# One decoder step on one core: the page stream pinned to its program order, and the second output projection moved in between FFN slices

## The chip, the core and the metric

The kernel runs on one core of one Trainium2 chip. The metric is the device time of one launch in microseconds (us). TensorE (PE in the profile, PEld for its weight loads), VectorE (DVE), ScalarE (ACT), GpSimd (POOL) and the DMA queue of SyncE (SP) each work through their own instruction stream in order and wait for each other by semaphores.

## The reference

One layer of a hybrid decoder, for a prompt of 1024 tokens and for 8 sequences of 8 new tokens each, which also attend to 8192 cached tokens. In short (widths: model 1024, FFN 2816):

```python
def layer_forward(h, p, pos, gla_s0, conv_prev, attend, lw):
    u = rmsnorm(h, lw['g_mix']) @ lw['w_in']
    gq, gk, gv, gg, ga, mq, mkv, mkr = split(u)
    ...                                        # o_gla: gated linear attention, 4 heads
    ckv = rmsnorm(mkv, lw['mla_g_kva']); krope = rope(rmsnorm(mkr, lw['mla_g_kr']), pos)
    k_m, v_m = latent_to_kv(ckv, krope, ...)   # 8 heads, per-head norm of the keys
    o_mla = attend(q_m, k_m, v_m)              # prompt: causal; sample: 64 cached pages of 128 per sequence
    h = h + concat([o_gla, o_mla]) @ lw['w_o']
    y, conv_new = conv_ffn(rmsnorm(h, lw['g_ffn']), conv_prev, lw)   # (silu(conv3(n @ gate)) * (n @ up)) @ down
    h = h + y
    return h + (p @ lw['ple_w_proj']) * sigmoid(rmsnorm(h, lw['g_ple']) @ lw['ple_w_gate']), ...
```

All data are float32. A product is made as three products of rounded halves (high x high, high x low, low x high; helper `mm3`), so that float32 precision is kept at the faster rate of the rounded type.

## The kernel before

The work has two strands. The **page stream** (`cache_stream`) is the sample sequences' attention over the cache: 64 blocks of 1024 cached tokens, eight for each sequence, called pages here. A page is gathered by indirect DMA (`stage_load`, two pages ahead, three buffers), transposed (`pre`, tile `ctp`, L518) and split into `cTh` and `cTl`; `main` multiplies it with the key weights and the queries (tile `ks`), ScalarE squares and copies the result out of PSUM (`csq`, `sn`); `stage_b` makes the key norm and the scores, `stage_c1` the softmax (`mt`, Exp, `phl`), `stage_pv` the product with the latents (`cpv`). The generator yields twice for each page, with half a page of `main` in each step, and `stage_b` of a page runs one page later, `stage_pv` two.

The **dense strand** (`dense`) is all else: input projections and latents in two halves of 512 prompt tokens (`prompt_half`), linear attention (`gla_sample`, `gla_prompt`), causal prompt attention (`prompt_attention`, tiles `S`, `t`, `o`), then for the first half of the prompt the output projection (`wo_half(0)`, sums in `ps_dn`) and the FFN (`ffn_half(0)`): 22 slices of 128 hidden columns, each with gate and up products (`ff_chunk`, tile `ps_gu`, 48 matmuls of 512 columns) and, for every two slices, the product with the down weights (`down`, 48 matmuls). Before the FFN the rows are normalised, transposed and split again (`renormer`: `row_scale`, `xnorm`, `turned`, tile `pt`).

A loop at the end of the program interleaves the strands in program order. The dense generator yields how many microseconds of TensorE it has just emitted; a step of the stream is emitted whenever the sum of these passes a due time, which each step moves on by 4.4 x `PACE[part]`. The parts are the projections (0 to 3), linear attention (4, 5), prompt attention (6), `wo_half(0)` (7) and the first FFN half (8). In the kernel before, the last step falls among the 22nd slice.

Program order is not the order that runs. At build time a scheduler places the instructions on the engines, by a simulated timeline: of what is ready, that which stands first in program order goes first, and later work may be pulled forward where an engine would otherwise be idle. `tc.keep_in_program_order(ins)` adds one constraint: `ins` is not placed ahead of the instruction that was traced before it on its engine.

After both strands have ended, the stream's memory is released and used for the second half's tiles (pools `psT` and `xr`: the rows `h1` and `hs`, the operand `X1`). Then come `wo_half(1)` (second half of the prompt and the sample rows; `down_sample`, tile `ps_ds`), its renormalisation, `ffn_half(1)` and the last gate (`ple_unit`). TensorE's sums take PSUM tiles in turn from `pd` (three banks) in the first half, and from `both` (`pd`, `pm`, `p2`, six banks) in the second.

Of the kernel before, what the change touches and what calls it, by code (L numbers as in the profile page):

```python
# [8 lines left out]
F32 = mybir.dt.float32  # L9
F32R = mybir.dt.float32r  # L10
# [5 lines left out]
PSUM = bass.MemoryType.PSUM  # L16
DRAM = bass.MemoryType.DRAM

P = 128
D = 1024  # L20
# [4 lines left out]
R = NB * TS  # L25
H = 8
DFF = 2816
PACE = [2.0, 1.5, 2.2, 1.65, 1.6, 1.0, 1.45, 1.37, 1.34]
SP = 50
PLAN = ([0], [], [1, 2, 3])  # L30
VIAP = 20
# [1 line left out]
VIAQ = 40  # L33
LOP = 1
NF = DFF // P
EPS = 1e-6
NEG = -1e30
SCALE = 96.0 ** -0.5
# [7 lines left out]
def step_kernel(ctx: ExitStack, tc: tile.TileContext, A):  # L46
    nc = tc.nc
    pe, act, dve, pool, sp = nc.tensor, nc.scalar, nc.vector, nc.gpsimd, nc.sync
# [9 lines left out]
    ident = ctile([P, P], F32, "ident")  # L58
# [119 lines left out]
    ph1 = ctx.enter_context(ExitStack())  # L178
# [18 lines left out]
    z = {}  # L197
# [310 lines left out]
    def pre(o, g0):  # L508
        buf = o.b % 2
        if g0 == 0:  # L510
            if o.bi == 0:
                seq_setup(o.b)
            o.sr = cp.tile([P, 9, 64], F32, tag="sr", name="sr", bufs=2)
        gn = min(4, o.nt - g0)
        craw = newc if g0 == 8 else o.craw[:, g0:g0 + 4]
        tp = pm([P, 4, P], "ctp")
        for i in range(gn):
            pe.transpose(tp[:, i, :], craw[:, i, :], ident)  # L518
        cTh = cp.tile([P, 4, P], F32R, tag="cTh", name="cTh", bufs=2)
# [792 lines left out]
    cs = cache_stream()  # L1312
    done = object()

    def dense():
        for hf in range(2):
            z["part"] = 2 * hf
            if hf:
                z["gla"] = gla_weights()
            yield from prompt_half(hf)  # L1320
        den.close()
        wa2 = const.tile([17, 256], F32, tag="gtile", name="wa2")
        sp.dma_start(wa2[0:1], A["gla_b_a"])
        sp.dma_start(wa2[1:17], A["gla_w_a2"][0])
        with ExitStack() as s2:
            g, g2 = (s2.enter_context(tc.tile_pool(name=nm, bufs=2, reuse_waits="tile")) for nm in ("g", "g2"))
            z["part"] = 4
            sample = gla_sample(g, wa2, *z["gla"])
            for n, w in enumerate(gla_prompt(g2, wa2, *z["gla"])):
                yield w  # L1330
                if n > GS0:
                    z["part"] = 5
                    w2 = next(sample, None)
                    if w2 is not None:
                        yield w2
            for w in sample:
                yield w
        gsx.close()
        with ExitStack() as s2:
            ap = s2.enter_context(tc.tile_pool(name="ap", bufs=2, reuse_waits="tile"))  # L1340
            z["part"] = 6
            yield from prompt_attention(ap)
        z["part"] = 7
        open_dense()
        yield from wo_half(0)
        z["part"] = 8
        yield from ffn_half(0)


    chunks, wgu = {}, {}  # L1350
# [3 lines left out]
    def open_dense():  # L1354
# [29 lines left out]
    def hrows(t):  # L1384
        return z["h"][t // 4][:, t % 4] if t < NT else z["hs"]
# [9 lines left out]
    def down(grp, bank, hf, after=None):  # L1395

        for t in range(4):
            tt = slice(t * P, (t + 1) * P)
            for f in range(2):
                cs = slice(f * 512, (f + 1) * 512)  # L1400
                ps = bank([P, 512], "ps_dn")
                for i, c in enumerate(grp):
                    sh, sl, _, wdh, wd = chunks[c]
                    mm3(ps, sh[:, tt], sl[:, tt], wdh[:, cs], wd[:, cs], i == 0, i == len(grp) - 1)
                h = hrows(4 * hf + t)[:, cs]
                dve.tensor_tensor(h, h, ps, ALU.add)  # L1406
            if after is not None:
                after(4 * hf + t)
            yield 2.7
# [15 lines left out]
    def row_scale(t):  # L1425
# [4 lines left out]
        for f, s_ in enumerate((s0, s1)):  # L1430
# [3 lines left out]
        pool.tensor_tensor(z["rs"][:rows, t:t + 1], s0, mhalf[:rows, 0:1], ALU.pow)  # L1434

    XN = {(False, 0): "sca", (False, 1): "cca", (False, 2): "guh", (False, 3): "gul",
          (False, 4): "cca", (False, 5): "sca", (False, 6): "guh", (False, 7): "gul", (False, 8): "pth",
          (True, 0): "pth", (True, 1): "ptl", (True, 2): "pth", (True, 3): "ptl",
          (True, 4): "cca", (True, 5): "guh", (True, 6): "cca", (True, 7): "gul", (True, 8): "cca"}

# [40 lines left out]
    def renormer(again, bank, lag=2):  # L1481

        last = []

        def step(t):
            if len(last) == lag or (t is None and last):
                turned(*last.pop(0), bank, again)
            if t is None:
                return
            row_scale(t)  # L1490
            xn = xn_halves(t, again)
            xnorm(t, xn, pool if (VIAQ if again else VIAP) >> t & 1 else dve)
            last.append((t, xn))
        return step
# [21 lines left out]
    def wo_half(hf):  # L1516

        bank = z["both"] if hf else pd
        if hf:
            sp.dma_start(z["hs"], A["x_sample"].rearrange("b t d -> (b t) d"))  # L1520
        for t in range(4 * hf, 4 * hf + 4):
            sp.dma_start(hrows(t), A["x_prompt"][0, t * P:(t + 1) * P, :])
        for g in range(4):
            grp = (2 * g, 2 * g + 1)
            for c in grp:
                wo_chunk(c, hf)
            if g == 0 and not hf:
                conv_weights()
                sp.dma_start(z["gb"], A["g_ffn"][0].partition_broadcast(P))
            if g == 1 and hf:  # L1530
                conv_state()
            if hf:
                down_sample([chunks[c][2:] for c in grp], bank)
            step = renormer(False, p2t if hf else pd) if g == 3 else None
            if g == 3:
                ff_weights(0, hf)
                if hf:
                    step(NT)
            yield from down(grp, bank, hf, step)
        step(None)  # L1540
        step(None)


    def columns(src, kc, lo_eng=None):
# [2 lines left out]
    def ff_weights(f, hf):  # L1547
        fs = slice(f * P, (f + 1) * P)
        wgu[f] = tuple(columns(A[nm][0][:, fs], 8, pool if not hf and nm == "ffn_w_up" or f < LOP else dve)
                       for nm in ("ffn_w_gate", "ffn_w_up"))  # L1550
# [63 lines left out]
    def ffn_half(hf, hooks={}):  # L1614
        bank = z["both"] if hf else pd
        for g in range(0, NF, 2):
            for f in (g, g + 1):
                yield from ff_chunk(f, hf)
            after = hooks[g]() if g in hooks else None
            yield from down((g, g + 1), bank, hf, after)  # L1620
            if hf:
                down_sample([chunks[c][2:] for c in (g, g + 1)], bank)

    dn = dense()
# [12 lines left out]
    ph1.close()  # L1637


    psT = ctx.enter_context(tc.tile_pool(name="psT", bufs=2, space=PSUM, reuse_waits="tile"))  # L1640

    def p2t(shape, name):
        return psT.tile(shape, F32, tag="t", name=name)

    def p2(shape, name):
        return psT.tile(shape, F32, tag="b", name=name, bufs=1)

    turn = [0]

# [2 lines left out]
        return (pd, pm, pd, pm, pd, p2)[turn[0]](shape, name)  # L1652

    z["both"] = both
    xr = z["xr"] = ctx.enter_context(tc.tile_pool(name="xr", bufs=1, side="right", reuse_waits="tile"))
    wf, fb, fw = z["wf"], z["fb"], z["fw"]
    z["h"].append(xr.tile([P, 4, D], F32, name="h1"))
    z["X"].append(xr.tile([P, 8, 2, 512 + R], F32R, name="X1"))
    hs = z["hs"] = xr.tile([R, D], F32, name="hs")
    cout = z["cout"] = xr.tile([P, 18, NF], F32, name="cout")  # L1660

    def gain(nm):
        sp.dma_start(z["gb"], A[nm][0].partition_broadcast(P))
# [1 line left out]
    def run(it):  # L1665
        for _ in it:
            pass
# [41 lines left out]
    def ple_gate(c):  # L1709
# [28 lines left out]

    hooks = {8 + 2 * t: early(t) for t in range(4)}
    hooks[NF - 2] = last_hook  # L1740
    run(ffn_half(1, hooks))
    step = steps[1]
    step(NT)

# [109 lines left out]
```

## Time and profile before

| what | value |
|---|---|
| median of 3 runs | 2309.7 us (2306.23 to 2310.57) |
| profiled execution | 2310.78 us, span 2309.1 us |
| granted TensorE clock, mean | 0.985 |
| busy: TensorE, VectorE, ScalarE, GpSimd | 2205.9, 1567.9, 1403.6, 1023.9 us |
| DMA | 207.67 MB, mean 90 GB/s |

The profile shows one execution. A matmul's duration there is its time in the pipeline; consecutive ones overlap, so that their rate is read from counts in a stretch, not from the mean duration. The granted clock is the share of TensorE's full clock that the chip allowed in a stretch.

### The profile page before, as it was taken

To read this page: it belongs to the slowest core of one execution; us is meant where nothing else is said; L and a number is where in the kernel's file an instruction comes from. 1 tells how busy PE (TensorE), PEld (TensorE's weight loads), DVE (VectorE), ACT (ScalarE), POOL (GpSimd) and SP (SyncE) were. 2 spreads that over 40 slices of the span, in tenths; PEclk is the share of its full clock that TensorE was granted. 3 is DMA by queue.
4 is the path that set the end of the run, shared out by engine and by line. 5 is a ranking of instruction groups with operands and counts; after the bars stand their busy time and mean duration, and the time that the engine had idled before them with its cause. 6 is when DMAs were issued, how large, how long until landed. Compare 5 with 4: busy or idle time off the path is not lost.

```text
span 2309.1 us, 38976 instructions
## 1 busy us (share of the span) xinstructions
PE 2205.9 (96%) x13855; PEld 1952.7 (85%) x13855; DVE 1567.9 (68%) x2590; ACT 1403.6 (61%) x3758; POOL 1023.9 (44%) x1223
## 2 busy tenths in 40 slices
PE   7999999999999999999999999999798999999999
PEld 6889888788888888878788888878667999999999
DVE  5765684778878788878755666666677656666642
ACT  6666666768788888876655467767635323232431
POOL 6665675766867777664532234444313000000100
PEclk9999999999999999999999999999898999999999
DMA  5343343323322122143332232222142223232131
GB/s 185 110 133 112 102 152 124 100 69 96 95 75 64 58 58 60 40 143 110 90 93 85 85 100 79 78 78 67 39 138 74 85 81 91 75 92 74 52 116 39
DMA packets 228531, 207.67 MB, mean 90 GB/s; under 512 B 41326, under 2 KB 190291, under 8 KB 228339
## 3 DMA queue, kind: packets, MB, share of 16 engines
q1 hardware_dynamic: 216051, 163.23, 23.5%
q0 software_dynamic: 12288, 41.95, 5.8%
q8 instruction: 111, 1.82, 0.3%
q14 instruction: 81, 0.66, 0.1%
HBM read 178.56 MB, written 26.53 MB: 89 GB/s over the span
## 4 chain that ended last, share of the span: by engine, by line
PE 54%; ACT 5%; DVE 5%; DMA 4%; POOL 3%; issue 2%; POOLq 0%; SPq 0%; DVEq 0%; ACTq 0%
PE ps_gu L137 6%; PE ps_gu L138 6%; PE ps_gu L139 6%; PE ps_dn L137 4%; PE ps_dn L138 4%; PE ps_dn L139 4%; PE ks L137 3%; PE ks L139 2%; PE ks L138 2%; PE ps_pg L139 1%; PE ps_pg L137 1%; PE ps_pg L138 1%; PE cpv L605 1%; PE ctp L518 1%; DMA stg<-ffn_w_gate 1%
## 5 line engine op out<-in xcount | busy, mean ns | idle before, releaser
L542 ACT ACTIVATE csq<-ks 128x256 f32<-128x256 f32 x1040 | 389.2, 400 | 91.1 <-PE ks L139 85.1
L547 DVE TENSOR_REDUCE css<-csq 128x16 f32<-128x1024 f32 (+1 forms) x264 | 315.9, 1197 | 81.0 <-ACT csq L542 75.4
L138 PE MATMUL ps_gu<-X,guh 128*128 128x320 f32 (+2 forms) x1056 | 349.0, 331 | 0.0
L139 PE MATMUL ps_gu<-X,gul 128*128 128x320 f32 (+2 forms) x1056 | 348.4, 330 | 0.0
L137 PE MATMUL ps_gu<-X,guh 128*128 128x320 f32 (+2 forms) x1056 | 348.3, 331 | 0.1
L137 PE MATMUL ks<-mv0h,cTh 128*128 128x256 f32 (+1 forms) x780 | 249.2, 320 | 10.6 <-ACT sn L544 7.3
L138 PE MATMUL ks<-mv0l,cTh 128*128 128x256 f32 (+1 forms) x780 | 225.8, 291 | 0.0
L139 PE MATMUL ks<-mv0h,cTl 128*128 128x256 f32 (+1 forms) x780 | 222.4, 292 | 0.0
L139 PEld LDWEIGHTS ps_gu<-X,gul 128*128 128x128 f32 x1056 | 199.9, 189 | 14.4
L138 PEld LDWEIGHTS ps_gu<-X,guh 128*128 128x128 f32 x1056 | 199.7, 189 | 14.6
L137 PEld LDWEIGHTS ps_gu<-X,guh 128*128 128x128 f32 x1056 | 199.3, 189 | 15.0 <-ACT X L116 0.4
L116 ACT CAST guh<-stg 128x512 fp32r<-128x512 f32 x188 | 111.4, 620 | 149.2 <-PE ps_gu L138 70.4
L137 PE MATMUL ps_dn<-wdh,sh 128*128 128x512 f32 x480 | 188.4, 400 | 3.6 <-DVE h L1406 2.6
L138 PE MATMUL ps_dn<-wdl,sh 128*128 128x512 f32 x480 | 189.1, 394 | 0.0
L139 PE MATMUL ps_dn<-wdh,sl 128*128 128x512 f32 x480 | 179.7, 395 | 0.0
L1406 DVE TENSOR_TENSOR h<-h,ps_dn 128x512 f32<-128x512 f32 x240 | 154.4, 680 | 34.3 <-PE ps_dn L139 33.9
L137 PEld LDWEIGHTS ks<-mv0h,cTh 128*128 128x128 f32 x780 | 148.1, 190 | 33.2 <-ACT sn L544 16.6
L574 POOL TENSOR_TENSOR chl<-craw,chl 128x1024 fp32r<-128x1024 f32 x64 | 141.8, 2215 | 62.7 <-ACT chl L573 62.1
L117 DVE TENSOR_TENSOR gul<-stg,guh 128x512 fp32r<-128x512 f32 x138 | 94.5, 708 | 101.3 <-ACT guh L116 97.6
L138 PEld LDWEIGHTS ks<-mv0l,cTh 128*128 128x128 f32 x780 | 148.3, 190 | 7.8 <-issue 1.3
L593 POOL TENSOR_TENSOR phl<-sn,phl 128x512 fp32r<-128x512 f32 (+1 forms) x64 | 85.8, 1340 | 147.5 <-ACT phl L592 147.3
L139 PEld LDWEIGHTS ks<-mv0h,cTl 128*128 128x128 f32 x780 | 145.8, 189 | 1.2
(556 smaller groups left out, 6302.4 us busy)
## 6 DMA issues: line engine op xcount, KB each, us to landing
stg<-ffn_w_gate SPq DMA_DIRECT2D x88, 256.0 KB
stg<-ffn_w_up SPq DMA_DIRECT2D x88, 256.0 KB
stage<-ffn_w_down SPq DMA_DIRECT2D x88, 256.0 KB
stage<-w_in SPq DMA_DIRECT2D x48, 256.0 KB
stage<-w_o SPq DMA_DIRECT2D x32, 256.0 KB
h<-x_prompt SPq DMA_DIRECT2D x8, 512.0 KB
oraw<-doT SPq DMA_DIRECT2D x16, 256.0 KB
stg<-ple_w_gate SPq DMA_DIRECT2D x16, 256.0 KB
```

Of the source, the lines that this page charges most:

```text
L116: act.copy(hi, src)
L117: (lo_eng or dve).tensor_tensor(lo, src, hi.bitcast(F32), ALU.subtract)
L137: pe.matmul(ps, ah, bh, start=first, stop=False)
L138: pe.matmul(ps, ah, bl, start=False, stop=False)
L139: pe.matmul(ps, al, bh, start=False, stop=last)
L518: pe.transpose(tp[:, i, :], craw[:, i, :], ident)
L542: act.activation(sq[:, f * 256:f * 256 + 256], ks[:, 0:256], AF.Square)
L547: dve.tensor_reduce(o.ss[:, g0 + i + 1 - n:g0 + i + 1, :].rearrange("p i h -> p (i h)"), sq2[:, :n].rearrange("p i (h n) -> p (i h) n", n= ...
L574: pool.tensor_tensor(ch[:, c0:c1, 128:256], src, ch[:, c0:c1, 0:128].bitcast(F32), ALU.subtract)
L593: pool.tensor_tensor(phl[:, :nt, 64:128], sb, phl[:, :nt, 0:64].bitcast(F32), ALU.subtract)
L605: pe.matmul(pv[:, 0:258], phl[:, i, :], o.ch[:, i, :], start=i == 0, stop=i == nt - 1)
L1406: dve.tensor_tensor(h, h, ps, ALU.add)
```

## The change

1. In `pre`, the first of the four transposes of every half page (those of cached pages, not of the new tokens) is kept in program order.
2. `PACE` is made smaller in all parts but one, so that in program order the stream's last step falls within FFN slice 17 (counted from 0) instead of slice 21.
3. The first FFN half is emitted as slices 0 to 17; then the rest of the stream, if any (`z["drain"]`); then the release of the stream's memory (`second_pools`, called when the stream ends); then `wo_half(1)`; then slices 18 to 21, with their down sums in the six banks of `both`. `wo_half(1)` no longer loads the weights of the second half's slice 0, and no longer finishes the renormalisation: its last blocks are transposed after `wo_half(1)` and after slices 20 and 21 (`z["step"](None)`).
4. The renormalised rows of the second half go to other buffers (`XN`): `ptl` and `pth` in place of `sca`, `cca`, `guh` and `gul`, which the FFN slices use.

```diff
-PACE = [2.0, 1.5, 2.2, 1.65, 1.6, 1.0, 1.45, 1.37, 1.34]
+PACE = [1.8, 1.35, 1.8, 1.45, 1.4, 1.0, 1.36, 1.25, 1.25]
+LASTG = 18
...
-            pe.transpose(tp[:, i, :], craw[:, i, :], ident)
+            ins = pe.transpose(tp[:, i, :], craw[:, i, :], ident)
+            if i == 0 and g0 < 8:
+                tc.keep_in_program_order(ins)
...
-        yield from ffn_half(0)
+        yield from ffn_half(0, range(0, LASTG, 2))
+        z["drain"] = True
+        yield 0.0
+        yield from wo_half(1)
+        z["step"](None)
+        for g in range(LASTG, NF, 2):
+            for f in (g, g + 1):
+                yield from ff_chunk(f, 0)
+                if g == NF - 2:
+                    z["step"](None)
+            if g == NF - 2:
+                ff_weights(0, 1)
+            yield from down((g, g + 1), both, 0)
...
-          (False, 4): "cca", (False, 5): "sca", (False, 6): "guh", (False, 7): "gul", (False, 8): "pth",
+          (False, 4): "ptl", (False, 5): "pth", (False, 6): "ptl", (False, 7): "pth", (False, 8): "pth",
...
-            step = renormer(False, p2t if hf else pd) if g == 3 else None
+            step = None
             if g == 3:
-                ff_weights(0, hf)
+                step = z["step"] = renormer(False, p2t if hf else pd)
                 if hf:
                     step(NT)
+                else:
+                    ff_weights(0, hf)
             yield from down(grp, bank, hf, step)
-        step(None)
-        step(None)
+        if not hf:
+            step(None)
+            step(None)
...
-        if live_c and (not live_d or due <= tdense):
+        if live_c and (not live_d or due <= tdense or "drain" in z):
             due += 4.4 * PACE[z["part"]]
             live_c = next(cs, done) is not done
             ncache += 1
+            if not live_c:
+                second_pools()
...
-    run(wo_half(1))
```

More of the change, by code (lines that the diff above doesn't have):

```diff
@@ L1514, in conv_state, with wo_half @@
         z["prv"] = prev.rearrange("p (b j f) -> p f b j", b=8, j=2)
-    def wo_half(hf):
+    def wo_half(hf, pairs=range(4)):
         bank = z["both"] if hf else pd
[L1519 to L1523, printed above, removed]
+        if pairs[0] == 0:
+            if hf:
+                sp.dma_start(z["hs"], A["x_sample"].rearrange("b t d -> (b t) d"))
+            for t in range(4 * hf, 4 * hf + 4):
+                sp.dma_start(hrows(t), A["x_prompt"][0, t * P:(t + 1) * P, :])
+        for g in pairs:
             grp = (2 * g, 2 * g + 1)
@@ L1612, in ff_chunk, with ffn_half @@
         chunks[f] = (sh, sl, ss_) + wdown(A["ffn_w_down"][0][fs, :])
-    def ffn_half(hf, hooks={}):
+    def ffn_half(hf, groups=range(0, NF, 2), hooks={}):
         bank = z["both"] if hf else pd
-        for g in range(0, NF, 2):
+        for g in groups:
             for f in (g, g + 1):
@@ L1622, in ffn_half, with p2t, p2, both @@
                 down_sample([chunks[c][2:] for c in (g, g + 1)], bank)
+    def p2t(shape, name):
+        return z["psT"].tile(shape, F32, tag="t", name=name)
+    def p2(shape, name):
+        return z["psT"].tile(shape, F32, tag="b", name=name, bufs=1)
+    turn = [0]
+    def both(shape, name):
+        turn[0] = (turn[0] + 1) % 6
+        return (pd, pm, pd, pm, pd, p2)[turn[0]](shape, name)
+    z["both"] = both
+    def second_pools():
+        ph1.close()
+        z["psT"] = ctx.enter_context(tc.tile_pool(name="psT", bufs=2, space=PSUM, reuse_waits="tile"))
+        xr = z["xr"] = ctx.enter_context(tc.tile_pool(name="xr", bufs=1, side="right", reuse_waits="tile"))
+        z["h"].append(xr.tile([P, 4, D], F32, name="h1"))
+        z["X"].append(xr.tile([P, 8, 2, 512 + R], F32R, name="X1"))
+        z["hs"] = xr.tile([R, D], F32, name="hs")
+        z["cout"] = xr.tile([P, 18, NF], F32, name="cout")
     dn = dense()
@@ L1636, in step_kernel @@
             tdense += w if live_d else 0.0
[L1637 to L1648, printed above, removed]
-    def both(shape, name):
-        turn[0] = (turn[0] + 1) % 6
[L1652 to L1660, printed above, removed]
+    xr, wf, fb, fw, hs, cout = (z[k] for k in ("xr", "wf", "fb", "fw", "hs", "cout"))
     def gain(nm):
@@ L1740, in step_kernel @@
     hooks[NF - 2] = last_hook
-    run(ffn_half(1, hooks))
+    run(ffn_half(1, hooks=hooks))
     step = steps[1]
```

## The prediction

> **What bounds the kernel now.** I read the page's totals first, then the busy time by stage, then the same table for the page stream's key matmuls (`ks`), then single waits. The stages: projections to 400 us, linear attention (GLA) to 605, prompt attention to 1003, its hand-over to 1027, first output projection and renormalisation to 1120, first FFN half to 1655, the end of the stream to 1680, second output projection to 1730, its renormalisation to 1756, second FFN half and the rest.
>
> ```profile
> span 2309.1 us, 38976 instructions
> ## 1 busy us (share of the span) xinstructions
> PE 2205.9 (96%) x13855; PEld 1952.7 (85%) x13855; DVE 1567.9 (68%) x2590; ACT 1403.6 (61%) x3758; POOL 1023.9 (44%) x1223
> ```
> ```profile
> 0.00:400.00 400.00, 370.60 (x2273) 333.29 (x2273) 250.36 (x458) 258.59 (x768) 251.84 (x315) 0.97 0.42 130
> 400.00:605.00 205.00, 197.06 (x1480) 170.72 (x1478) 158.95 (x267) 155.29 (x515) 150.23 (x212) 1.00 0.34 95
> 605.00:1003.00 398.00, 385.85 (x2637) 336.83 (x2638) 321.12 (x534) 339.87 (x1008) 291.77 (x295) 1.00 0.21 60
> 1003.00:1027.00 24.00, 18.96 (x123) 15.57 (x121) 21.23 (x30) 20.17 (x63) 12.05 (x12) 1.00 0.67 230
> 1027.00:1120.00 93.00, 87.85 (x495) 76.12 (x496) 76.03 (x119) 64.22 (x182) 48.98 (x53) 0.96 0.34 105
> 1120.00:1655.00 535.00, 524.22 (x2708) 440.52 (x2707) 358.38 (x506) 341.88 (x776) 195.57 (x185) 1.00 0.27 82
> 1655.00:1680.00 25.00, 10.49 (x48) 8.09 (x47) 6.31 (x16) 7.39 (x14) 5.92 (x5) 0.59 0.26 94
> 1680.00:1730.00 50.00, 46.86 (x200) 35.85 (x198) 40.29 (x64) 18.77 (x36) 5.63 (x6) 1.00 0.35 109
> 1730.00:1756.00 26.00, 14.76 (x88) 12.84 (x88) 19.75 (x25) 19.74 (x51) 15.96 (x23) 0.74 0.17 52
> 1756.00:2309.00 553.00, 549.22 (x3814) 522.88 (x3814) 315.53 (x578) 177.71 (x353) 45.92 (x120) 1.00 0.26 79
> ```
>
> The columns are the stretch, its length, then busy time of PE, PEld, DVE, ACT and POOL, the granted clock, DMA share and GB/s. TensorE bounds every stage but two short ones: 1655 to 1680 and 1730 to 1756. They are what the change goes for. The stream, by the same stages:
>
> ```profile
> 0.00:400.00 400.00, 101.28 (x571) 0.97 0.42 130
> 400.00:605.00 205.00, 96.00 (x552) 1.00 0.34 95
> 605.00:1003.00 398.00, 188.23 (x1042) 1.00 0.21 60
> 1003.00:1027.00 24.00, 14.42 (x81) 1.00 0.67 230
> 1027.00:1120.00 93.00, 30.68 (x170) 0.96 0.34 105
> 1120.00:1655.00 535.00, 119.20 (x708) 1.00 0.27 82
> ```
>
> A page has 48 `ks` matmuls (eight tiles, two column groups, three products) and two steps of the stream's generator. Prompt attention therefore saw 1042 / 48 = 21.7 pages, 43 steps. The program emits far fewer there: a step falls due every 4.4 x PACE of the dense yields, and attention's yields sum to 154.9, so 154.9 / (4.4 x 1.45) = 24 steps. The scheduler pulled some 19 steps, nine or ten pages, forward out of the FFN, as filling. The same count for the stages to 400 us gives 25 emitted against 571 / 24 = 24 seen: there the stream is on its program place. This difference decides the case, because the change forbids it.
>
> **Prices.** A 512-column matmul:
>
> ```profile
> 1203.00:1219.00 16.00, 16.00 (x70) 1.00 0.42 132
> ```
>
> These are `ps_gu` alone, 16.00 / 70 = 0.229 us each. The first FFN half holds 22 x 48 = 1056 of them and 11 x 48 = 528 of `ps_dn`, 363 us; its stage lasts 535 and is idle for 10.8. So 14.75 pages (708 / 48) took 535 - 363 - 11 = 161 us, 10.9 us a page with its small waits. The stretch 1003 to 1027, nearly all stream, gives 18.96 / 1.69 = 11.2. I take 10.9, 5.4 a step, in every stage; then steps that are moved between stages cost nothing by themselves.
>
> **The end of the stream (removed wait).**
>
> ```profile
> 1655.80 1.12 PE L605 MATMUL cpv<-chl,phl 128*128 128x258 f32 x8
> 1664.80 0.48 PE L581 MATMUL mt<-ident,ml 128*128 128x128 f32 x1 [7.87 <-POOL ml L569]
> ...
> 1669.96 2.09 PE L605 MATMUL cpv<-chl,phl 128*128 128x258 f32 x8 [3.49 <-POOL phl L593]
> 1674.38 0.34 PE L627 MATMUL pt_ol<-ident,acclo 64*128 64x64 f32 x1 [2.33 <-DVE acclo L625]
> ```
> ```profile
> SPq L1520 <- PE cpv L605: 20.1, 1, 20.1
> ```
> ```profile
> 1676.00:1680.00 4.00, 4.00 (x17) 2.94 (x16) 1.13 (x3) 1.31 (x3) 0.00 (x0) 0.52 1.02 410
> 1680.00:1684.00 4.00, 3.62 (x17) 2.66 (x16) 3.90 (x7) 0.58 (x1) 0.00 (x0) 1.00 0.02 7
> ```
>
> The last page's softmax is a serial chain over five engines, and `x_sample` and `x_prompt` rows can only be loaded once its last product has freed the memory (SP waits 20.1 us, with all later weight loads behind it). Idle in 1655 to 1756 is 14.5 + 3.1 + 11.2 = 28.8 us; what ran at clocks of 0.59 and 0.74 lost another (10.49 x 0.41) + (14.76 x 0.26) = 8.1. Together 37 us. After the change FFN slices 18 to 21 stand behind `wo_half(1)` in program order and need nothing of it: 4 x 48 + 2 x 48 = 288 matmuls, 66 us, to cover 29 us of idle. Slice 18's gate and up products (11 us) fit under the softmax chain; their `wd` buffers (two) and the SP queue behind `x_sample` limit what more can go. The renormalisation (26 us) lies under slices 19 to 21; its rows now go to `pth` and `ptl`, so it takes no FFN buffer. I leave 7 us: the price of the change is **-30** here, between -37 and -10 (if `wo_half(1)`'s blocked sums hold the PSUM banks that slice 18 wants).
>
> The Trainium skill ("TensorE: Matmul & The Clock Gate", Part 1) says that after an idle window of about 3.4 us TensorE runs at half clock until it has been busy for as long. The trace agrees (0.52, then 1.00, above), and so the same rule bills every hole that the change opens elsewhere; without it the terms below would be some 2 us less.
>
> **The pin (added wait).** The first transpose of each half page now stays behind the last TensorE instruction traced before it, which is nearly always a dense matmul. Queued behind the pinned transpose are that half page's `cTh`, its `ks`, scores and sums; dense work is not. So the stream can never be ahead of program order by more than the step in hand, 5.4 us of TensorE. Where dense work waits longer, TensorE now waits too. With the new PACE the emission is 29, 19, 26, 8 and 52 steps (projections, GLA, attention, first output projection, 18 FFN slices), sum over 4.4 x PACE each. Holes, one by one:
>
> ```profile
> 1002.62 0.44 PE L1281 MATMUL o<-pl,vo 128*128 128x512 f32 x1
> ```
> ```profile
> 1027.40 0.48 PE L137 MATMUL ps_dn<-wdh,sh 128*128 128x512 f32 x1
> ```
>
> (1) From attention's last matmul to the first output projection 24.8 us pass: the last division, then loads of rows and weights at 230 GB/s. Stream work of 81 `ks` (3.4 steps) covers it now, 5.0 us idle. After it, one step is emitted ahead of the last sums, and the next is pinned behind the second block of `ps_dn`. 24 - 5.4 = 18.6 idle instead of 5.0: +13.6, and a cold restart like that of 1676 to 1680 (4 us at 0.52, so 1.9): **+15**.
>
> (2) Smaller hand-overs: into GLA, where
>
> ```profile
> 400.00:440.00 40.00, 21.37 (x123) 17.05 (x123) 16.28 (x63) 1.00 0.49 133
> ```
>
> shows 5 steps (123 / 24) against 3 emitted up to there, into attention, and from the renormalisation into FFN slice 0. Two steps of cover less at the first, one at each other, 21 us at most; I take **+13**, nearer the upper end because the hand-over above is all load latency, which does not close up.
>
> (3) Inside attention: 398 us held 21.7 pages (237 us), so 161 us are its own. With 26 steps it needs 161 + 13 x 10.9 = 303 if its own pace closes up. I add **+12** for the turns between its 16 items, about 0.75 us each; bounds are 0 and 398 - 303 = 95 (it keeps the old pace).
>
> (4) Below nothing: in-order transposes could remove waits of the stream itself:
>
> ```profile
> L137 PE MATMUL ks<-mv0h,cTh 128*128 128x256 f32 (+1 forms) x780 | 249.2, 320 | 10.6 <-ACT sn L544 7.3
> ```
>
> at most these 10.6 us. I take 0, for the waits are for ScalarE's evictions, not for pages.
>
> **ScalarE in the FFN.** 26 pages now fall among 18 slices instead of 14.75 among 22, and Silu and Ln/Exp reload tables in turn:
>
> ```profile
> L1601 ACT ACT_TABLE_LOAD x16 | 20.5, 1283 | 0.3
> L556 ACT ACT_TABLE_LOAD x15 | 19.2, 1283 | 0.3
> L557 ACT ACT_TABLE_LOAD x13 | 16.7, 1283 | 0.2
> L598 ACT ACT_TABLE_LOAD x11 | 14.1, 1283 | 0.2
> ```
>
> A page brings 39 / 14.75 = 2.6 loads, so 11.25 pages bring 30 more, 38 us. A page's other ScalarE work is 20.17 / 1.69 = 11.9 us (1003 to 1027), 134 us. With four slices out (their share of what is no page's: (341.9 - 70.5 - 14.75 x 11.9) x 4 / 22 = 17 us) ScalarE needs 342 + 38 + 134 - 17 = 497 us of a stage of 18 x 72 x 0.229 + 26 x 10.9 = 580: 86%, as in attention now (339.87 of 398), where TensorE still sets the pace. So nothing is added; without that cover it would cost what it exceeds. The Trainium skill ("ScalarE: Activation LUTs", What ACT_TABLE_LOAD costs) counts a drain of 1.38 us beside each load; this trace shows 1283 ns a load and 0.2 to 0.3 us of idle before all loads of a row, so I go by the trace. By the skill's figure, an estimate, 85 loads x 1.38 would add 117 us and make ScalarE the bound of the stage, 34 us longer, 2355 in all.
>
> Everything else moves without changing: `wo_half(1)`'s 192 `ps_dn`, its DMAs on SP, conversions and `conv_state` run in the same order among themselves, now ahead of four slices' weights.
>
> **Sum.** The profiled execution took 2310.78 us (span 2309.1; the median of the runs is 2309.7, so it stands for them). 2310.8 - 30 + 15 + 13 + 12 = **2321 us**, 0.5% slower. A measurement of this kernel can tell about 0.2%, 4.6 us.
>
> **Rivals.** (A) The pin seldom binds: the stream lags its program place, as it does a little to 400 us (24 of 25), so 3.4 steps are still in hand when attention ends and the holes are filled as now. Then only the end counts: 2310.8 - 30 + 5 = **2286**. It decides from a backlog of 18 us of stream at the hand-over. For it speaks that attention shares four engines with the stream and gains speed as the stream thins; against it that the stream ran 19 steps ahead, so dense work was what waited. (B) The end keeps its hole, as the blocked sums hold PSUM: -10 instead of -30, **2341**. This is also the case in which the change does not do what it says. (C) An engine behind TensorE becomes the bound: attention keeps its pace of now, which is its own chain through ScalarE and GpSimd and not the stream's competition. At 398 us it adds 83, at half of that the time is **2362**. It decides if fewer than 15 pages run in more than 330 us. ScalarE in the FFN, at 86% by the rows, belongs here too: its full bound gives 2321 until it exceeds 580 us, which takes 65 more loads.
>
> **How the numbers follow.** Forecast 0.45, A 0.33, B 0.12, C 0.10. Of the forecast (2306 to 2336 by its own) 0.03 falls below 2306, 0.08 within 0.2%, the rest above; of A 0.31 and 0.02. Faster 0.34, same 0.11, slower 0.55. The range takes in A and B and half of C: 2280 to 2352.
>
> **What would show it.** Right: no `ks` between about 1010 and the first `ps_dn`, with a granted clock near 0.5; some 13 pages in attention, 26 from the first `ps_gu`; no idle over 5 us after the stream's last `cpv`, `ps_gu` of 512 columns beside it; FFN slice 0 of the second half starting without a `pt` wait. Wrong: `ks` counts in attention near 1000 still, the hand-over filled, or ScalarE over 95% in the FFN.

## The result and the profile after

The changed kernel takes 2413.59 us (2411.50 to 2414.32), the kernel before beside it on the same chip 2307.97: a ratio of 1.0456, 95% interval 1.0438 to 1.0474. The forecast was 2321 with a range to 2352, so the sign was right and the size was not: 106 us instead of 10. The sign came from added waits, as forecast; the end of the stream, which was to give 30 us back, took longer.

The totals of the page after: the same 13855 matmuls, a span 101 us longer, and a TensorE that is busy for 93% of it instead of 96%. The mean granted clock fell from 0.985 to 0.970.

```profile
span 2409.8 us, 38991 instructions
PE 2248.7 (93%) x13855; PEld 1974.9 (82%) x13855; DVE 1566.7 (65%) x2590; ACT 1436.1 (60%) x3775; POOL 1026.7 (43%) x1223
```

The busy time by stretch of the changed kernel, cut at the first or last matmul of each stage or part of one (columns as in the prediction: stretch, length, busy PE, PEld, DVE, ACT, POOL, granted clock, DMA share, GB/s). The rows are the projections, GLA, attention, hand-over, first output projection, FFN slices 0 to 17, the first blocks of `wo_half(1)`, the stream nearly alone, `wo_half(1)`, slices 18 to 21, second FFN half and rest:

```profile
0.00:423.00 423.00, 388.25 (x2393) 350.72 (x2393) 264.81 (x481) 278.41 (x829) 266.62 (x331) 0.97 0.41 128
423.00:636.00 213.00, 197.07 (x1400) 167.95 (x1400) 145.13 (x254) 144.68 (x462) 140.96 (x201) 0.95 0.30 86
636.00:975.00 339.00, 315.35 (x1988) 260.57 (x1986) 244.25 (x409) 255.90 (x715) 220.70 (x225) 0.96 0.19 53
975.00:996.00 21.00, 5.47 (x38) 4.62 (x36) 10.90 (x15) 11.12 (x27) 7.43 (x6) 0.79 0.65 234
996.00:1093.00 97.00, 91.83 (x522) 79.37 (x523) 79.88 (x117) 64.63 (x187) 44.74 (x50) 0.96 0.31 95
1093.00:1579.00 486.00, 464.94 (x2512) 394.64 (x2511) 327.19 (x468) 341.39 (x811) 203.65 (x201) 0.99 0.26 79
1579.00:1600.00 21.00, 20.91 (x123) 18.11 (x121) 16.92 (x29) 14.30 (x39) 6.29 (x6) 1.00 0.16 49
1600.00:1718.00 118.00, 86.43 (x477) 73.29 (x475) 64.40 (x95) 87.00 (x234) 50.36 (x43) 0.82 0.13 37
1718.00:1780.00 62.00, 56.66 (x245) 44.12 (x246) 45.62 (x77) 23.00 (x47) 4.14 (x4) 0.95 0.42 134
1780.00:1851.00 71.00, 66.85 (x307) 53.12 (x306) 46.27 (x66) 34.11 (x71) 26.23 (x32) 1.00 0.34 101
1851.00:2410.00 559.00, 554.98 (x3864) 528.39 (x3862) 321.35 (x584) 181.61 (x365) 55.57 (x128) 1.00 0.26 79
```

The kernel before, cut at the same events (to FFN slice 0, slices 0 to 17, from there to the second FFN half, rest):

```profile
0.00:407.00 407.00, 376.30 (x2312) 338.38 (x2312) 256.06 (x466) 264.32 (x789) 258.67 (x326) 0.97 0.43 132
407.00:613.00 206.00, 198.97 (x1494) 172.22 (x1494) 160.25 (x272) 156.00 (x509) 149.47 (x206) 1.00 0.33 92
613.00:1003.00 390.00, 378.23 (x2582) 330.24 (x2582) 314.11 (x520) 333.43 (x991) 285.70 (x291) 1.00 0.21 58
...
1119.00:1506.00 387.00, 382.82 (x1939) 320.83 (x1937) 255.42 (x361) 236.50 (x522) 138.93 (x135) 1.00 0.29 87
1506.00:1744.00 238.00, 204.74 (x1044) 167.97 (x1043) 162.40 (x241) 146.09 (x343) 79.66 (x79) 0.93 0.25 80
1744.00:2309.00 565.00, 558.99 (x3880) 532.21 (x3878) 323.43 (x587) 183.76 (x366) 50.81 (x127) 1.00 0.26 78
```

Stage by stage: projections +16, GLA +7, attention -51, hand-over -3, first output projection +5, slices 0 to 17 +99, from there to the second FFN half 272 (21 + 118 + 62 + 71) against 238, +34, rest -6: together 101 us. The `ks` matmuls say what moved (48 a page), first of the changed kernel, then of the one before:

```profile
636.00:975.00 339.00, 113.59 (x651) 96.03 (x651) 87.03 (x330) 0.96 0.19 53
975.00:996.00 21.00, 3.92 (x24) 3.29 (x24) 3.29 (x13) 0.79 0.65 234
1093.00:1579.00 486.00, 140.12 (x801) 119.90 (x800) 105.88 (x399) 0.99 0.26 79
1579.00:1600.00 21.00, 7.28 (x45) 6.65 (x45) 6.05 (x24) 1.00 0.16 49
1600.00:1718.00 118.00, 57.76 (x282) 46.80 (x282) 37.25 (x143) 0.82 0.13 37
```
```profile
613.00:1003.00 390.00, 185.28 (x1024) 152.23 (x1025) 138.08 (x516) 1.00 0.21 58
1119.00:1506.00 387.00, 74.93 (x436) 66.04 (x436) 57.70 (x219) 1.00 0.29 87
```

Attention lost 7.8 pages (1024 to 651) and got only 51 us shorter; slices 0 to 17 gained 7.6 (436 to 801) and got 99 us longer. After slice 17, 5.9 pages (282) run for 118 us with next to nothing beside them, 20 us a page. In that stretch SP's queue stands still. Its waits (total, times, longest) and its issues (start, duration) in the changed kernel:

```profile
SPq L668 <- POOL chl L577: 42.5, 1, 42.5
SPq L668 <- DMA craw<-cache_ckv,idx: 35.2, 1, 35.2
SPq L1536 <- PE cpv L608: 33.1, 1, 33.1
```
```profile
1606.05 0.33 SPq L1405 DMA_DIRECT2D oraw<-doT  x1
1684.26 0.63 SPq L668 DMA_DIRECT2D WvT<-mla_w_kvup  x1
1718.07 0.52 SPq L1536 DMA_DIRECT2D hs<-x_sample  x1
```

`WvT` takes a page buffer and waits for the last pages; `hs` waits for the last `cpv`. For 112 us this queue loads nothing else, and what stands behind in it includes the rest of `wo_half(1)` and the weights of slice 18.

### The profile page after: what moved, and what is told of

It is laid out like the page before. It is cut to its first block, busy times and chain, and to the rows that moved or that the text cites. A ratio compares the mean times of both kernels' runs of the same rounds, so it can differ in the third digit from the quotient of the medians.

```text
span 2409.8 us, 38991 instructions
## 1 busy us (share of the span) xinstructions
PE 2248.7 (93%) x13855; PEld 1974.9 (82%) x13855; DVE 1566.7 (65%) x2590; ACT 1436.1 (60%) x3775; POOL 1026.7 (43%) x1223
## 4 chain that ended last, share of the span: by engine, by line
PE 53%; ACT 10%; DVE 7%; DMA 4%; POOL 3%; issue 3%; SPq 0%; ACTq 0%; POOLq 0%; DVEq 0%
PE ps_gu L138 5%; PE ps_gu L139 5%; PE ps_gu L140 5%; PE ps_dn L138 4%; PE ps_dn L139 3%; PE ps_dn L140 3%; PE ks L138 3%; PE ks L139 3%; PE ks L140 2%; DMA stg<-ffn_w_gate 2%; ACT csq L545 2%; PE cpv L608 2%; PE ps_pg L140 1%; PE ps_pg L138 1%; PE ps_pg L139 1%
```

## The experiments

### The pin, the pace and the order, apart

E1 takes out the pin of the changed kernel.

```diff
-            ins = pe.transpose(tp[:, i, :], craw[:, i, :], ident)
-            if i == 0 and g0 < 8:
-                tc.keep_in_program_order(ins)
+            pe.transpose(tp[:, i, :], craw[:, i, :], ident)
```

> The changed kernel with its one pin taken out; the new pace and the new order stay. Theory T1 (the pin is the cause: the stream cannot run ahead, every wait of the dense strand becomes idle TensorE, and the losses add up to a backlog of some six pages that has to run alone after slice 17): the waits are filled again, attention sees about 20 pages (over 950 ks) instead of 14.7, the stream ends with slice 17 or before it, and the time falls by 100 to 130 us, to 2285-2315. Theory T2 (the new order is the cause: wo_half(1) stands ahead of slices 18 to 21, its sums take the PSUM banks while they wait for rows, and nothing can run beside the stream's end): the start to slice 17 gets its 70 us back or less, but a stretch of 40 us or more with ks, no ps_gu and an idle TensorE stays ahead of wo_half(1); 2340-2360.

E2 puts these lines into the kernel before, E3 these lines and the new `PACE`, E4 the new `PACE` alone.

> The kernel before with the pin alone (old pace, old order). T1: the added waits by stage in the changed kernel (start +14, GLA +15, attention +25, hand-over +8, FFN +10) come back here, 72 us, and the end gets worse as well if a backlog is left after slice 21: 2370-2420. T2: the pin costs only what the forecast gave it, 40 us at most: 2320-2350, and the end looks as before.

> The kernel before with the pin and the new pace; the order is the old one (22 slices, then wo_half(1)). The stream's last step then stands in slice 17 and four slices of dense work follow that need nothing new. T1: start to slice 17 costs 70 us more as in the changed kernel, but the backlog of six pages runs beside slices 18 to 21, so the 120 us of stream alone go and the end looks as before: 2370-2385. T2: 2320-2350. If a long stretch of stream alone appears here too (over 60 us), neither the order nor the banks made it.

> The kernel before with the new pace alone (no pin, old order). T1: the scheduler fills as before and the stream is only some steps earlier; it ends ahead of slice 21 with dense work beside its last softmax, so 5-15 us of the hole at the end may go; 2295-2312. Rival: the thinner spacing itself costs (the stream stands ahead of dense work in program order more often and delays attention's own chain): 2320-2350, with longer waits of t, o and S.

Measured, as ratios to the kernel before: E1 1.0005 (0.9992 to 1.0019), E2 1.0507 (1.0476 to 1.0538), E3 1.0377 (1.0360 to 1.0395), E4 0.9959 (0.9942 to 0.9976). With 1% at 23 us: the pin costs 97 us (E3 against E4) or 104 (the changed kernel against E1). The new order costs 11 without the pin (E1 against E4) and 18 with it, where the forecast had a gain of 30. The pace gains 9 alone and 30 with the pin. Both theories hold in part. T1 holds for nearly all of the loss: without the pin attention sees 1018 `ks` again. T2 holds for the end: in E1 the stream still runs on for 62 us behind slice 17 with no `ps_gu` beside it, and the new order brings nothing. E2 came out above T1's range, E1 at its upper end, and E3, 14 us above its range, has a late stream with the old order too.

E4 and E3 differ by the pin alone. Attention, slices 0 to 17, and from there to the second FFN half, first E4, then E3:

```profile
627.00:1017.00 390.00, 377.15 (x2558) 328.51 (x2557) 314.19 (x516) 328.42 (x979) 282.64 (x281) 0.99 0.21 58
...
1139.00:1555.00 416.00, 405.45 (x2102) 340.42 (x2102) 276.22 (x388) 268.30 (x601) 158.69 (x153) 1.00 0.28 85
1555.00:1735.00 180.00, 165.71 (x798) 133.18 (x797) 127.58 (x196) 103.19 (x227) 50.80 (x55) 0.97 0.30 92
```
```profile
638.00:977.00 339.00, 315.29 (x1987) 260.49 (x1986) 244.43 (x410) 256.20 (x715) 221.16 (x225) 0.96 0.19 53
...
1096.00:1582.00 486.00, 465.63 (x2516) 396.20 (x2515) 328.76 (x470) 342.58 (x814) 205.02 (x202) 0.99 0.27 81
1582.00:1831.00 249.00, 218.40 (x1131) 179.86 (x1130) 169.31 (x255) 158.29 (x379) 84.40 (x81) 0.93 0.25 77
```

And the `ks` matmuls of the same stretches, E4, then E3:

```profile
627.00:1017.00 390.00, 185.05 (x1017) 152.96 (x1017) 137.15 (x510) 0.99 0.21 58
...
1139.00:1555.00 416.00, 88.75 (x534) 78.45 (x534) 67.92 (x263) 1.00 0.28 85
1555.00:1735.00 180.00, 19.67 (x120) 17.37 (x120) 16.49 (x64) 0.97 0.30 92
```
```profile
638.00:977.00 339.00, 113.66 (x653) 95.92 (x651) 87.18 (x330) 0.96 0.19 53
...
1096.00:1582.00 486.00, 140.78 (x801) 120.72 (x801) 106.21 (x399) 0.99 0.27 81
1582.00:1831.00 249.00, 56.24 (x327) 48.95 (x327) 42.62 (x165) 0.93 0.25 77
```

This is the case in three divisions. Attention without 7.6 pages (1017 to 653) is 51 us shorter: a page there was worth **6.7 us**, on the average of these 7.6. (It is no constant: E2 had only 564 `ks` in attention and took 316 us there, against E3 some 12 us less for each page less.) Slices 0 to 17 with 5.6 more (534 to 801) are 70 us longer: **12.6 us** a page. Behind slice 17 it is 69 us for 4.3 pages (120 to 327), **16**. The pin moved pages from where they filled waits to where there are none.

### Where the pin costs

E6 and E7 are E4 with the pin on half pages emitted in one part alone; E8 is the kernel before with the pin everywhere and 46 steps of program order in attention.

```diff
 E6 +            if i == 0 and g0 < 8 and z["part"] == 6:
 E7 +            if i == 0 and g0 < 8 and z["part"] == 8:
 E8 +PACE = [2.0, 1.5, 2.2, 1.65, 1.6, 1.0, 0.77, 1.25, 2.2]
```

> The pace-only kernel (2302.4) with the pin on half pages that are emitted in prompt attention alone. The pin everywhere cost 97 us there. Theory T3 (the pin's price is local: it is paid in each stage by the waits that the stream can no longer fill): attention and its hand-over lose 25 us, the FFN takes up the seven pages at their plain price: 2322-2335. Theory T4 (the price is a lag: pages not run in attention fall to a place with less slack, and the stream ends late): 2340-2380, most of the loss behind slice 17.

> The pace-only kernel (2302.4) with the pin on half pages that are emitted in the FFN alone. T3: the FFN's slices run without the stream until the program place has caught up with its lead of some 20 steps, then as in the fully pinned kernel; slices 0 to 17 lose 10 to 20 us, attention and the hand-over nothing: 2310-2325. T4: the stream's lead of attention is thrown away, so it ends as late as in the fully pinned kernel, and the loss is 50 us or more: 2350-2400.

> The kernel before with the pin everywhere, and a pace that puts the steps where the free schedule ran them: 46 in attention instead of 26 (0.77), 37 in the FFN (2.2), the last in slice 21. T4 (the pin hurts because the program place was wrong by 20 steps): attention holds 21 pages again, the stream ends beside slice 21, and the time is within 30 us of the unpinned kernels: 2310-2340. T3 (the pin hurts because the free schedule fills waits too small and too irregular for any spacing): attention keeps an excess of 65 us or more, and the time stays above 2360.

Measured: E6 1.0274 (1.0249 to 1.0299), E7 1.0258 (1.0235 to 1.0280), E8 1.0220 (1.0198 to 1.0241). T3's prices were far too low; T4 holds for E6 and E7. Against E4 either part alone costs some 70 us (73 and 69), and all parts together 97: the costs do not add, as each takes away the same lead. E7 shows how. It pins nothing before the FFN, but the stream then uses up all steps emitted so far while attention runs, and has none left. The `ks` of E7 in attention, the hand-over and the first output projection:

```profile
626.00:998.00 372.00, 154.91 (x849) 128.00 (x849) 114.33 (x426) 0.97 0.20 56
998.00:1017.00 19.00, 0.00 (x0) 0.00 (x0) 0.00 (x0) 0.61 0.65 230
1017.00:1085.00 68.00, 0.00 (x0) 0.00 (x0) 0.00 (x0) 0.93 0.35 105
```

E8 against E2 (both with the pin everywhere and the old order) gets 66 us back by placing the steps where the free schedule had run them; 51 us over the kernel before stay. It is between T3 and T4: more than half of the pin's price in E2 is the place. The rest are waits that this spacing, the one that was tried, did not fill; 24 us of them stand before attention, which starts at 637 us instead of 613.

### What holds the end

E5 and E9 place `wo_half(1)` one pair of slices later, E5 without and E9 with the pin. E12 is E5 with a denser FFN pace. E10 is the changed kernel with what slice 18 shares with `wo_half(1)` taken away in part.

```diff
 E5, E9  -LASTG = 18
         +LASTG = 20
 E12     +PACE = [1.8, 1.35, 1.8, 1.45, 1.4, 1.0, 1.36, 1.25, 1.15]
 E10     +        ff_weights(LASTG, 0)
                  yield from wo_half(1)
         ...
         -        bank = z["both"] if hf else pd
         +        bank = z["off"] if hf else pd      # pm, pm, p2 in turn
```

> The changed kernel without the pin, and with wo_half(1) between slices 19 and 20 instead of 17 and 18. Theory U1 (slices that stand behind wo_half(1) can never run under the stream's end, because its sums and rows stand ahead of theirs in the rings of PSUM banks and buffers and in SP's queue; slices that stand ahead of it can): slices 18 and 19 now run beside the last softmax, 20 and 21 beside the renormalisation, and both short holes close. Against the pace-only kernel (2302.4) the 17 us of idle TensorE at the renormalisation go and nothing comes back: 2283-2293. Rival U2 (the new order costs of itself, by slices 20 and 21 on the wider set of banks or by the early release of the stream's memory): it stays at 2300-2315 with a new wait between last cpv and ps_ds or in slices 20 and 21.

> The changed kernel, pin kept, with wo_half(1) between slices 19 and 20. Theory U1 (what stands ahead of wo_half(1) can run beside the late stream, what stands behind it cannot): slices 18 and 19 (33 us of matmuls) now run beside some three of the six late pages, the stretch of stream alone shrinks from 120 us to 60-80, and 15-25 us come back: 2388-2400. Theory U3 (the late pages are bound by their own chain and take as long beside anything): the stream still ends near 1718 and the time stays at 2405-2415.

> The changed kernel, pin kept, with two edits that let slice 18's gate and up products pass wo_half(1): the weights of slice 18 are loaded ahead of its rows, and its sums take pm and p2 instead of pd, so that the slice's two banks stand before them in no ring. Theory U1 (rings and SP's queue held slice 18, not the scheduler's choice): 48 ps_gu of slice 18 run ahead of the last cpv, in the idle TensorE beside the stream's last pages, and up to their 11 us come back: 2400-2408. Rival: they run there but only take the place of ps_dn, or three banks less make wo_half(1) wait for VectorE's additions: 2411-2425.

> The unpinned kernel with wo_half(1) between slices 19 and 20 (2292.3) with the FFN's pace at 1.15 instead of 1.25, so that the last step stands about a slice and a half earlier. If the 8.7 us of idle TensorE left behind the last cpv there come from the stream ending too late for the rows, they go: 2283-2290. If the denser pace only moves waits (the stream runs ahead of its place anyway): 2290-2296.

Measured: E5 0.9934 (0.9912 to 0.9957), 16 us under E1; E9 1.0388 (1.0362 to 1.0414), 16 under the changed kernel; E10 1.0474 (1.0449 to 1.0498), no gain; E12 0.9941 (0.9923 to 0.9959), no gain. U1 is right for E5 and E9. E10 tells why slice 18 stayed behind: the `ps_gu` of the changed kernel in the stream's last stretch, then those of E10 from the end of slice 17 on.

```profile
1600.00:1718.00 118.00, 0.00 (x0) 0.00 (x0) 0.00 (x0) 0.00 (x0) 0.82 0.13 37
```
```profile
1583.00:1625.00 42.00, 12.48 (x50) 8.73 (x48) 1.37 (x2) 0.60 (x1) 1.00 0.20 60
1625.00:1725.00 100.00, 0.00 (x0) 0.00 (x0) 0.00 (x0) 0.00 (x0) 0.81 0.09 28
```

With its own banks and its weights loaded first, slice 18 (48 `ps_gu`) does pass the blocked projection; so sharing, not the scheduler's choice, held it. It brings nothing in time: it runs at once and leaves 100 us of the stream still uncovered, and `wo_half(1)` has three banks less; which of these weighs more is not shown. Which of the two edits slice 18 needed most wasn't run apart. E12 went nearly as its second reading had it (2297 us, that reading said 2290 to 2296): without the pin the FFN's pace decided nothing here.

### ScalarE's table loads

E11 (pinned) and E13 (E1, no pin) compute Square in place of SiLU. E16 is the changed kernel with one more table load behind each Silu, E14 the same on E5. E15 is E5 with the SiLU made of functions of one table set.

```diff
 E11, E13 +        act.activation(cv[:, :n], cv[:, :n], AF.Silu if hf else AF.Square)
 E14, E16  act.activation(cv[:, :n], cv[:, :n], AF.Silu)
          +if hf == 0:
          +    tc.keep_in_program_order(act.preload_act_table_set("natural_log_exp_and_others"))
 E15      +sg = a[:, 0:512]                                    # hf == 0 only
          +act.activation(sg, cv[:, :n], AF.Exp, scale=-1.0)
          +act.activation(sg, sg, AF.Ln, bias=one1)
          +act.activation(sg, sg, AF.Exp, scale=-1.0)
          +dve.tensor_tensor(cv[:, :n], cv[:, :n], sg, ALU.mult)
```

> The changed kernel with Square in place of Silu in the first half's FFN slices, which leaves the SiLU out of these slices: no table for Silu is loaded there any more, and fewer for Ln and Exp in turn. Theory W1 (a page costs 12.5 to 13.7 us in the FFN, not the 10.9 of the sum, because ScalarE's table loads delay its evictions): slices 0 to 17 shorten by 20-40 us from 486: 2365-2392. Theory W2 (the price comes from the page's own small waits on evictions, whatever the loads): slices 0 to 17 stay within 8 us and the time at 2403-2415; the stream's end, alone with Ln and Exp, changes in neither.

> The changed kernel without the pin (2312.1) and with Square in place of Silu in the first half's FFN slices, which leaves the SiLU out of them. In the pinned kernel that took 47 us. Theory V1 (the table loads are dear because of the pin: it put six more pages among the slices, and a pinned page waits for every eviction): here they cost 10-20 us: 2292-2302, and the pin itself still costs 65-75 us. Theory V2 (the loads cost the same in any order): 2262-2272, and the pin still costs its full 97-102 us.

> The changed kernel, pin kept, with the table set of Ln and Exp loaded right after each Silu of the first half. About 40 of its 80 loads go, all of Ln's and Exp's, and the stream's end has none. If the 47 us without Silu came from the loads that stand inside a page's chain: 25-40 of them come back here, 2375-2390. If Silu's own load and work were the cause: under 12 us, 2402-2412.

> The unpinned kernel with wo_half(1) between slices 19 and 20 (2292.3), and after each Silu of the first half one load of the table set that holds Ln and Exp together, so that Ln and Exp no longer load in turn (all arithmetic stays). 12 of its 61 loads go. If the loads' place matters (Ln and Exp stand in the page's serial chain, the load after Silu does not): 2278-2288. If only their number does, 12 x 1.28 = 15 us of ScalarE work at a TensorE that mostly does not wait for it: 2288-2294.

> The same unpinned kernel (2292.3) with the first half's SiLU made of Exp, Ln and Exp, all of one table set, and one more product on VectorE: no table load is left among the slices, 56 fewer than there, 72 us of ScalarE; the slices bring 20 x 2 x 0.63 = 25 us of Exp and Ln more. If table loads are what makes ScalarE's evictions late in the FFN: 2272-2284. If the longer chain of a slice (three operations and a product instead of one) holds up its down products instead: 2290-2300.

Measured: E11 1.0237 (1.0216 to 1.0258), 51 us under the changed kernel; E13 0.9947 (0.9926 to 0.9968), 13 under E1; E16 1.0330 (1.0314 to 1.0345), 29 under the changed kernel; E14 0.9957 (0.9943 to 0.9971), not told apart from E5; E15 0.9897 (0.9878 to 0.9916), the fastest: 24 us under the kernel before, 8 or 9 under E5 with intervals that just touch. W1 and V1 hold, and E16 lies in the range for loads inside a page's chain; E14 lies above both of its ranges and E15 short of its gain, so without the pin the loads have little left to give. Leaving out Silu takes away all loads but 5: 75 of 80 in E11, 53 of 58 in E13. So a load cost some 0.7 us in the pinned order and 0.25 in the free one. Silu's own work is not the cause: these activations take 29.0 us with Square too. One expectation failed: the stream's end was to stay, and it took 22 us less in E11 (from slice 17 to the second FFN half 250 us instead of 272); no load is left there either. Slices 0 to 17 of E11, then of E13:

```profile
1103.00:1560.00 457.00, 455.88 (x2518) 393.35 (x2517) 328.08 (x469) 270.77 (x753) 203.33 (x201) 1.00 0.28 84
```
```profile
1141.00:1546.00 405.00, 403.19 (x2104) 341.39 (x2104) 278.55 (x386) 210.70 (x555) 157.51 (x154) 1.00 0.28 85
```

With the same pages there as E3 and E4 (801 and 534 `ks`), the slices differ by 52 us for 5.6 pages: 9.3 us a page instead of 12.6, and TensorE is idle for 1 or 2 us in all. The other 3.3 us of a page in the FFN go with ScalarE's loads. In the changed kernel, slices 0 to 17 (`ACT_TABLE_LOAD`: count, busy, mean ns, idle before), then the same lines in the stretch where the stream is alone:

```profile
L1620 ACT ACT_TABLE_LOAD x17 | 21.8, 1283 | 5.3 <-DVE cv L1612 5.0
L559 ACT ACT_TABLE_LOAD x16 | 20.5, 1283 | 0.3
L560 ACT ACT_TABLE_LOAD x14 | 18.0, 1283 | 0.2
L601 ACT ACT_TABLE_LOAD x13 | 16.7, 1283 | 0.2
```
```profile
L559 ACT ACT_TABLE_LOAD x7 | 9.0, 1283 | 0.1
L560 ACT ACT_TABLE_LOAD x6 | 7.7, 1283 | 0.1
```

Sixty loads in 18 slices: Ln (L559) and Exp (L560) load in turn, even in the second stretch, where no Silu stands between them. The Trainium skill ("ScalarE: Activation LUTs", Table sets: the hidden batching unit) says that Ln followed by Exp takes one load, since one set holds both. The trace of the changed kernel differs: each loads its own. E16, which loads that common set by hand, has 49 loads in all instead of 80 and none at Ln or Exp, so the rule is right for the set and not for what stood in this program. In E11, where no Silu runs in these slices, none is left at Ln or Exp either, and nobody loads the set by hand; why they load in turn once a Silu has run was not looked into.

## Why the prediction was wrong, by its own steps

**Where the stream stood: right.** 13 pages were forecast for attention, 13.6 ran; no `ks` stands between 982 us and the first `ps_dn`, at a clock of 0.79.

**"I take 10.9, 5.4 a step, in every stage; then steps that are moved between stages cost nothing": the step that failed.** 10.9 is an average of one stage. What a move costs is the price at the margin, and that was 6.7 in attention, 12.6 in the FFN (E3 against E4) and 16 to 20 at the end. By these prices the 7.6 pages that leave attention for the slices would cost 45 us, where the forecast had nothing for the move itself, and more where they land behind the slices. In the terms below this is the miss in attention and in the slices, 22 and 16 us; the largest single miss, 46, is the end's.

**Attention, +12: mis-sized by 22.** From the kernel before to the changed one, 390 us with 1024 `ks` became 339 with 651. By 10.9 a page, 7.8 pages less are 85 us less; it got 51 shorter, so 34 us were added and not 12. Some of them are clock, which the forecast billed for the large hand-over alone: the granted clock was 0.96 instead of 1.00, by an estimate from the row 315 x 0.04 = 13 us. The rest are waits of attention's own chain that the stream no longer fills, which is argued and not shown. This is rival C, whose condition (fewer than 15 pages in more than 330 us) was met; the measured 34 lie about midway between the forecast's 12 and the 53 of C at half its bound (12 + 41).

**The end, -30: mis-sized by 46, two premises.** First, the 26 pages were all to run beside slices 0 to 17. 23.5 were left by then: 16.7 ran beside the slices, 6.8 behind them (45 `ks` to 1600 us, 282 after). Program order had given these steps their place, but nothing lets the stream make up a delay once a pin forbids it to run ahead. Second, slices 18 to 21 "need nothing of" `wo_half(1)`: they stand behind it in the banks, the buffers and SP's queue (E10), so none ran beside the last softmax. That was rival B's mechanism, priced at 20 us over the forecast; what it is worth alone is not shown, for E10 takes it away from slice 18 and gains nothing. By 10.9 a page the old order's 238 us, less 30, with 1.1 pages more, give 220; 272 were seen, 52 more, of which the rest of the kernel gave back 6. E3 shows that nearly all of this is the new order's: with the same pin and the same 327 `ks` behind slice 17, the old order took 249 us there and 567 for the rest, the new one 272 and 559. So it lost 15 us where it was to gain 30. What was right: the renormalisation is covered. The stretch 1780 to 1851 is busy for 66.85 of 71 us, and the second FFN half no longer waits for it (559 us for it and the rest, 565 before).

**Smaller hand-overs, +13: mis-sized by 12.** Projections and GLA together took 23 us more with 0.2 pages less (1131 `ks` against 1140), 25 by the forecast's price. Here too clock was left out: GLA ran at 0.95 instead of 1.00, by an estimate from the row 197 x 0.05 = 10 us.

**The large hand-over, +15: 4 too much.** The idle stretch ahead of `ps_dn` is there:

```profile
996.09 0.38 PE L1516 MATMUL pt_cv<-ident,cvec 88*128 88x88 f32 x1 [13.85 <-DMA cvec<-ffn_conv_b]
```

Hand-over and first output projection took 2 us more with 0.8 pages less, 11 by the forecast's price.

**ScalarE and the slices, +0: mis-sized by 16.** The rows had ScalarE at 86% and behind TensorE, so 0. It was 70% busy (341 of 486), no bound, and still its loads cost 51 us (75 loads) instead of the 13 (53 loads) of the free order: E11 and E13 show the price. The way is shown in part. In slices 0 to 17 the idle time of TensorE falls from 21 us to 1 without the loads; of the 21, some 7 are `ks` that wait for an eviction (`csq`, `sn`), and some 5 are `ps_dn` that wait for what follows a slice's Silu (`cv`, `sh`). That a pinned stream has no other page to go on with, and so pays more for a load, is argued. Against 10.9 a page this is 16 us: slices 0 to 17 took 99 us more for 7.6 pages, which are 83 at 10.9, and 10.9 already held the loads of the kernel before. The drain of 1.38 us a load that the Trainium skill ("ScalarE: Activation LUTs", What ACT_TABLE_LOAD costs) counts shows in none of these rows: 0.1 to 0.3 us of idle stand before the loads of Ln and Exp.

The sum of the misses: 22 + 46 + 12 + 16 - 4 = 92. The span grew by 101 us where the terms of the forecast add up to 10; the difference of 91 is the same but for rounding.

**The range** ended at 2352, below rival C's own 2362, and added no two rivals, although B and C could happen together. Even both, at their prices, give only 2321 + 20 + 41 = 2382. The chances have a slip as well: by their parts "same" adds up to 0.10 and "slower" to 0.56, not 0.11 and 0.55.

## What to carry to other kernels

Price filler work at the margin of the stage it leaves and of the stage it enters, by two traces or two stretches with different densities, never by one average: the same page cost 6.7 us where TensorE had waits to fill and 12.6 where it had few. A constraint that only holds work back turns each small wait into a lag that nothing recovers; no run here found a place for the pin that was free (even before attention it cost 11 us, E3 against E4). Moving a consumer of late memory ahead of independent work can block that work through the rings and queues that they share. Cover a wait with work that stands ahead of it: `wo_half(1)` one pair of slices later, with no pin, made the kernel 0.7% faster, and with a SiLU of one table set besides 1.0%.

## What was not expected of the hardware

Loads of 1283 ns each, in a kernel with 60% of ScalarE busy, were worth 51 us of device time in one instruction order (75 loads) and 13 in another (53 loads). And Ln and Exp reloaded in turn 13 times in 118 us with no Silu between, until the set that holds both was loaded by hand.
